# Seven conditioning vectors computed as fp32 products on TensorE instead of multiply-adds on VectorE

## The chip, the cores and the metric

One Trainium2 chip, one core of it. The metric is the device time of one execution in microseconds, smaller is better. A difference is told from no change at about 0.2%, some 4 us here.

## The reference, cut to what matters

One layer of a diffusion backbone over 1024 latent tokens and 256 context tokens, model width 1024. A conditioning vector c and a context vector c_ctx each pass through silu and one matrix `w_ada` (1024 x 9216) and give nine vectors of 1024, which shift, scale and gate the three sub-layers:

```python
def adaln(cond, w, b):
    m = jax.nn.silu(cond) @ w + b
    return [t[..., None, :] for t in jnp.split(m, N_MOD, axis=-1)]

def half_step_ffn(x, mods, g_pre, g_post, w_gu, w_down):
    shift, scale, gate = mods
    h = modulate(rms_norm(x, g_pre), shift, scale)
    g, u = jnp.split(h @ w_gu, 2, axis=-1)
    y = (jax.nn.silu(g) * u) @ w_down
    return x + 0.5 * gate * rms_norm(y, g_post)
...
        mods = adaln(c, w_ada[i], b_ada[i])
        mods_c = adaln(c_ctx, w_ada[i], b_ada[i])
        x = half_step_ffn(x, mods[0:3], ...)
        ctx = half_step_ffn(ctx, mods_c[0:3], ...)
        # mixer: x uses mods[3:6], ctx uses mods_c[3:5]
        x = half_step_ffn(x, mods[6:9], ...)
```

Everything is fp32. A layer of c_ctx needs vectors 0 to 4 only, one of c needs all nine.

## The kernel before

The stages follow each other in time: the first up product of the latent tokens (`g_lat`, to about 512 us), the same of the context (`g_ctx`), the two down products (`d_lat`, `d_ctx`, to about 1060 us), the mixer (in-projection, S5 scans, convolution, out-projection, to about 1510 us), the second up product (`g_lat` again, 1510 to 1920 us) and its down product. An operand of a large product is split into a high and a low fp32r half by ScalarE (a copy) and VectorE (a subtraction); three fp32r products of 512 columns then make one fp32 product. The up products use a seven-product scheme: each of 22 column blocks of the weight takes 7 x 12 matmuls, 1848 in all, and VectorE makes the sums and differences and the low halves that they need.

Vectors 0 and 1 of c are made at the start, by code of their own. The others come from `ada_mods` (line 327), a generator that runs as filling work: `step` (line 122) takes some of its yields at fixed points of a large product and issues them at lower priority. For each vector and each of 8 row blocks of `w_ada` (512 KB, loaded into a ring of five slots named tb, two blocks ahead) `ada_acc` multiplies the block on VectorE by a column of silu(c) (the tile scol) and adds it to an accumulator of 128 x 1024, once for c and once for c_ctx. `ada_col` then sums over partitions: a VectorE transpose in 32 x 32 pieces, a VectorE reduction (the tile red), one small fp32 product with a fixed matrix sel, and four VectorE adds of the bias into the column tile mod. For a gate vector `ada_gate` transposes that column on TensorE and sends it out as a row.

Vectors 1 to 4 are filling work of the first up product, followed by `s5_params` (small VectorE and GpSimd work for the mixer); 5 and 6 of the first down products (`fill56`), 7 of the mixer, 8 of the second up product. The order of the instructions on each engine is set when the program is built, by a list scheduler with its own timing estimates; VectorE is held to the written order only in the opening. Each engine runs its instructions in order, so one that waits holds up those behind it. In the profile nearly all instructions carry line 51, that of a recording helper; they are told apart by tile names. ps is a PSUM tile, w an operand half, wr a raw weight block, z, t and tb are working tiles.

Of the kernel before, what the change touches and what calls it, by code (L numbers as in the profile page):

```python
# [13 lines left out]
OP = mybir.AluOpType  # L14
# [54 lines left out]
class Kernel:  # L69
# [110 lines left out]
    def setup(self):  # L180
# [40 lines left out]
        nc.vector.tensor_copy(self.scol, pt[:, :16])  # L221
        self.ones = self.t(cp, [P, 1], "ones")
        nc.gpsimd.memset(self.ones, 1.0)
        self.modc = {}

    def selector(self):

        nc, cp = self.nc, self.cp
        red = self.t(cp, [P, 32], "red")
        nc.vector.tensor_reduce(  # L230
            red, self.ident.rearrange("p (a j) -> p j a", j=32), axis=AX.X, op=OP.add
        )
        self.sel = self.t(cp, [P, P], "sel")
        for a in range(4):
            nc.vector.tensor_copy(self.sel[:, 32 * a : 32 * a + 32], red)
# [46 lines left out]
    def ada_col(self, acc, mod, cond):  # L282
        nc = self.nc
        tmp = self.ta()
        nc.vector.transpose(tmp, acc)
        red = self.t(self.cp, [P, 32], f"red{mod}_{cond}")
        nc.vector.tensor_reduce(
            red, tmp.rearrange("p (b j) -> p b j", j=32), axis=AX.X, op=OP.add
        )
        self.td_(tmp)  # L290
        yield
        pt = self.ps()
        nc.tensor.matmul(pt[:, :32], self.sel, red, start=True, stop=True)
        col = self.t(self.cp, [P, KT], f"mod{mod}_{cond}")
        for q in range(4):
            r = slice(32 * q, 32 * q + 32)
            self.add(
                col[r, :],
                pt[r, :32].rearrange("p (k q) -> p q k", q=4)[:, q, :],
                self.b_ada(mod)[r, :],  # L300
            )
        self.modc[mod, cond] = col
        yield
# [23 lines left out]
    def ada_mods(self, plan, look=2):  # L327
# [3 lines left out]
        for p, (n, kt) in enumerate(seq):  # L331
# [4 lines left out]
            if kt == 0:  # L336
                accs = [self.ta() for _ in conds]
            w = ws.pop(0)
            for a, cond in zip(accs, conds):
                self.ada_acc(a, w, kt, cond)  # L340
            self.td_(w)
            yield
            if kt == KT - 1:
                self.td_(*accs)
                for a, cond in zip(accs, conds):
                    yield from self.ada_col(a, mod, cond)
# [1266 lines left out]
    def run(self):  # L1613
# [102 lines left out]
        self.selector()  # L1716
# [12 lines left out]
        def fill():  # L1729
            for _ in range(FW):  # L1730
# [6 lines left out]
                (4, (1, 0), scales4),  # L1737
            ])
# [43 lines left out]
        def fill56():  # L1782
            for _ in range(DW):
                yield
# [248 lines left out]
SF = (15, 1)  # L2033
TY = 4
FC = 2
DW = 0
FW = 34
FN = 3
UN2 = 3
# [47 lines left out]
```

## Time and profile before

| | us |
|---|---|
| median of 3 runs (2123.9 to 2125.89) | 2124.05 |
| the profiled execution's own time | 2125.93 |
| span of its trace | 2124.2 |
| TensorE matmul busy in the span | 1925.3 (91%) |
| VectorE busy | 1636.0 (77%) |
| ScalarE busy | 817.0 (38%) |

PE is TensorE, PEld its weight loads, DVE VectorE, ACT ScalarE, POOL GpSimd, SP the queue that issues nearly all DMAs. The busy time of PE counts the modelled end of each matmul, so that 91% does not say how much room TensorE has; that is read from the number of matmuls in a stretch and their spacing. A matmul whose operands are plain fp32 leaves two records in the trace, an fp32r one leaves one; a TensorE transpose leaves one.

### The profile page before, as it was taken

What the parts mean: (1) busy time and instruction counts of PE and PEld (TensorE: products, weight loads), DVE (VectorE), ACT (ScalarE), POOL (GpSimd) and SP (SyncE); (2) the same over time, 40 slices, a digit from 0 to 9 for tenths busy, and PEclk for the clock granted to TensorE, in tenths of its full rate; (3) what the DMA queues carried; (4) which work ended last, traced back from release to release, by engine and by line L of the source; (5) the groups of instructions that cost most, each with busy time, mean ns of one, the idle gap of its engine ahead of it and who ended that gap; (6) DMA issues with size and microseconds to landing.
All of it is one profiled execution on the core that took longest, in us unless ns stands there. A gap on an engine that the chain in (4) does not pass through costs nothing.

```text
span 2124.2 us, 25468 instructions
## 1 busy us (share of the span) xinstructions
PE 1925.3 (91%) x9018; PEld 1594.7 (75%) x9018; DVE 1636.0 (77%) x2813; ACT 817.0 (38%) x1416; POOL 229.5 (11%) x136
## 2 busy tenths in 40 slices
PE   5779998898899988999997779998899999998997
PEld 4568776686899866877886668886688888886876
DVE  6689998998766699598549998478875555579867
ACT  5433322333343333566531113347233333333543
POOL 0000000041337100000003552010000000000000
PEclk9889999999999999999999899999899999999999
DMA  8347552344579969367684433233552322267754
GB/s 299 95 145 245 160 184 84 88 150 139 172 241 264 320 226 339 128 229 279 186 235 174 153 127 114 72 104 114 182 175 79 99 80 90 70 226 250 243 169 168
DMA packets 338444, 366.21 MB, mean 172 GB/s; under 512 B 43216, under 2 KB 250764, under 8 KB 338316
## 3 DMA queue, kind: packets, MB, share of 16 engines
q1 hardware_dynamic: 336012, 356.19, 51.6%
q10 hardware_dynamic: 2304, 8.39, 1.0%
q8 instruction: 71, 1.16, 0.2%
q14 instruction: 57, 0.47, 0.1%
HBM read 299.22 MB, written 67.35 MB: 173 GB/s over the span
## 4 chain that ended last, share of the span: by engine, by line
PE 54%; DVE 29%; DMA 8%; issue 4%; ACT 2%; POOL 2%; SPq 1%; DVEq 0%; ACTq 0%; POOLq 0%
PE ps L51 54%; DVE t L51 10%; DVE z L51 6%; DVE w L51 5%; DVE tb L51 5%; DMA wr<-in_ffn_w_down 2%; DMA tb<-in_w_ada 2%; POOL z L51 1%; SPq L51 1%; DMA wr<-in_ffn_w_gu 1%; DMA z<-in_w_ada 1%; ACT z L51 1%; ACT w L51 1%; DMA wr<-t2d 1%; ACT t L51 0%
## 5 line engine op out<-in xcount | busy, mean ns | idle before, releaser
L51 PE MATMUL ps<-z,w 128*128 128x512 f32 (+1 forms) x5712 | 1245.9, 379 | 94.4 <-ACT w L51 46.1
L51 PEld LDWEIGHTS ps<-z,w 128*128 128x128 f32 x5712 | 1020.8, 194 | 296.1 <-ACT w L51 52.5
L51 PE MATMUL ps<-w,w 128*128 128x512 f32 x1848 | 439.3, 397 | 29.9 <-DVE w L51 23.9
L51 PEld LDWEIGHTS ps<-w,w 128*128 128x128 f32 x1848 | 348.4, 191 | 117.5 <-DVE w L51 35.0
L51 ACT ACTIVATE w<-wr 128x512 fp32r<-128x512 f32 (+1 forms) x308 | 228.9, 747 | 378.8 <-PE ps L51 287.0
L51 DVE TENSOR_TENSOR w<-wr,w 128x512 fp32r<-128x512 f32 (+1 forms) x302 | 268.6, 894 | 91.1 <-ACT w L51 83.6
L51 ACT ACTIVATE w<-t 128x512 fp32r<-128x512 f32 x264 | 160.2, 626 | 294.0 <-DVE t L51 255.6
L51 DVE TENSOR_TENSOR w<-t,w 128x512 fp32r<-128x512 f32 x264 | 181.1, 699 | 40.9 <-ACT w L51 40.6
L51 DVE TENSOR_TENSOR t<-t,ps 128x512 f32<-128x512 f32 x150 | 102.2, 683 | 66.0 <-PE ps L51 65.6
L51 ACT ACTIVATE w<-z 128x512 fp32r<-128x512 f32 x132 | 83.3, 631 | 161.1 <-PE ps L51 158.4
L51 DVE TENSOR_TENSOR w<-z,w 128x512 fp32r<-128x512 f32 x132 | 90.8, 688 | 48.0 <-ACT w L51 47.8
L51 ACT ACTIVATE t<-ps 128x512 f32<-128x512 f32 (+2 forms) x135 | 73.7, 548 | 99.7 <-PE ps L51 98.0
L51 DVE TENSOR_TENSOR z<-z,z 128x512 fp32r<-128x512 f32 (+3 forms) x127 | 103.8, 852 | 9.6 <-ACT z L51 5.8
L51 DVE SCALAR_TENSOR_TENSOR tb<-tb,scol 128x1024 f32<-128x1024 f32 x77 | 97.9, 1280 | 8.6 <-DMA tb<-in_w_ada 8.4
L51 DVE TENSOR_TENSOR t<-wr 128x512 f32<-128x512 f32 x126 | 85.4, 685 | 16.7 <-DMA wr<-in_ffn_w_gu 11.1
L51 POOL TENSOR_TENSOR z<-z,z 128x1024 f32<-128x1024 f32 x24 | 85.4, 3576 | 76.4 <-PE ps L51 39.8
L51 ACT ACTIVATE t<-z 128x1024 bf16<-128x1024 f32 (+3 forms) x132 | 75.2, 605 | 44.3 <-DVE z L51 32.1
L51 ACT ACTIVATE t<-t 128x512 f32<-128x512 f32 (+1 forms) x81 | 50.6, 625 | 104.1 <-DVE t L51 100.1
L51 PE MATMUL ps<-z,t 128*128 128x512 f32 x384 | 87.8, 389 | 1.1 <-ACT t L51 1.1
L51 PEld LDWEIGHTS ps<-z,t 128*128 128x128 f32 x384 | 72.0, 188 | 16.4 <-ACT t L51 1.5
L51 POOL TENSOR_TENSOR tb<-tb 128x512 f32<-128x512 f32 x24 | 33.8, 1422 | 451.3 <-DVE w L51 431.0
L51 ACT ACTIVATE z<-z 128x512 fp32r<-128x512 f32 (+2 forms) x76 | 47.9, 672 | 78.6 <-DVE z L51 72.5
(124 smaller groups left out, 1447.6 us busy)
## 6 DMA issues: line engine op xcount, KB each, us to landing
wr<-in_ffn_w_gu SPq DMA_DIRECT2D x156, 512.0 KB, 4.1
wr<-in_ffn_w_down SPq DMA_DIRECT2D x242, 256.0 KB, 4.4
tb<-in_w_ada SPq DMA_DIRECT2D x64, 512.0 KB, 5.0
sd<-z SPq DMA_DIRECT2D x44, 512.0 KB, 4.8
z<-sd SPq DMA_DIRECT2D x88, 256.0 KB, 5.6
z<-in_w_ada SPq DMA_DIRECT2D x24, 512.0 KB, 6.1
wr<-in_ffn_w_down SPq DMA_DIRECT2D x22, 512.0 KB, 3.6
wr<-in_w_in SPq DMA_DIRECT2D x20, 512.0 KB, 4.0
```

The lines of the kernel that those rows point to most:

```text
L51: r = f(*a, **kw)
```

## The change

Vectors 1 to 4 of c_ctx and 2 to 8 of c are no longer summed on VectorE. A new tile `srep` holds, for each of the 8 row blocks, silu(c) and silu(c_ctx) side by side, repeated 16 times to 32 columns. For each block of `w_ada` TensorE makes four fp32 products of 256 columns, with those 32 columns as the stationary operand; the four write to partitions 0, 32, 64 and 96 of one PSUM tile, so that each uses another group of 32 columns of the array, and accumulate over the 8 blocks. One product serves c and c_ctx at once. `ada_col` copies the result to SBUF on ScalarE, transposes it twice on TensorE and adds the bias in one VectorE instruction per vector. The transposes of 1024 columns, the reductions and `sel` are gone, and with `fill56` and the filling work of the mixer vectors 5, 6 and 7 move into the filling work of the first up product, ahead of `s5_params`. Eight blocks of each of these eight vectors are 256 products there; vector 8 has 32 in the second up product.

```diff
--- before.py
+++ after.py
@@ -219,20 +219,14 @@
         self.tr(pt[:, :16], srow, 16)
         self.scol = self.t(cp, [P, 16], "scol")
         nc.vector.tensor_copy(self.scol, pt[:, :16])
+        self.srep = self.t(cp, [P, KT, 32], "srep")
+        nc.scalar.activation(
+            self.srep.rearrange("p k (n c) -> p n c k", c=2),
+            pt[:, :16].rearrange("p (c k) -> p c k", c=2).unsqueeze(1).to_broadcast([P, 16, 2, KT]), AF.Copy,
+        )
         self.ones = self.t(cp, [P, 1], "ones")
         nc.gpsimd.memset(self.ones, 1.0)
         self.modc = {}
-
-    def selector(self):
-
-        nc, cp = self.nc, self.cp
-        red = self.t(cp, [P, 32], "red")
-        nc.vector.tensor_reduce(
-            red, self.ident.rearrange("p (a j) -> p j a", j=32), axis=AX.X, op=OP.add
-        )
-        self.sel = self.t(cp, [P, P], "sel")
-        for a in range(4):
-            nc.vector.tensor_copy(self.sel[:, 32 * a : 32 * a + 32], red)
 
     def consts(self):
         nc, i, cp = self.nc, self.i, self.cp
@@ -279,27 +273,21 @@
         else:
             self.stt(acc, w, s, acc, OP.mult, OP.add)
 
-    def ada_col(self, acc, mod, cond):
-        nc = self.nc
-        tmp = self.ta()
-        nc.vector.transpose(tmp, acc)
-        red = self.t(self.cp, [P, 32], f"red{mod}_{cond}")
-        nc.vector.tensor_reduce(
-            red, tmp.rearrange("p (b j) -> p b j", j=32), axis=AX.X, op=OP.add
-        )
-        self.td_(tmp)
+    def ada_col(self, pt, mod, conds):
+        rows = self.t2([P, 256])
+        self.nc.scalar.activation(rows, pt[:, :256], AF.Copy)
         yield
         pt = self.ps()
-        nc.tensor.matmul(pt[:, :32], self.sel, red, start=True, stop=True)
-        col = self.t(self.cp, [P, KT], f"mod{mod}_{cond}")
-        for q in range(4):
-            r = slice(32 * q, 32 * q + 32)
+        for b in range(2):
+            self.tr(pt[:, b * P : b * P + P], rows[:, b * P : b * P + P], P)
+        for cond in conds:
+            col = self.t(self.cp, [P, KT], f"mod{mod}_{cond}")
             self.add(
-                col[r, :],
-                pt[r, :32].rearrange("p (k q) -> p q k", q=4)[:, q, :],
-                self.b_ada(mod)[r, :],
+                col.rearrange("p (j b) -> p j b", b=2),
+                pt[:, : 2 * P].rearrange("p (b j r) -> p j b r", b=2, j=4)[:, :, :, cond],
+                self.b_ada(mod).rearrange("p (j b) -> p j b", b=2),
             )
-        self.modc[mod, cond] = col
+            self.modc[mod, cond] = col
         yield
 
     def ada_scale(self, mod, cond, k):
@@ -334,16 +322,17 @@
                 q, k = seq[p + len(ws)]
                 ws.append(self.ada_load(plan[q][0], k, self.ta()))
             if kt == 0:
-                accs = [self.ta() for _ in conds]
+                pt = self.ps()
             w = ws.pop(0)
-            for a, cond in zip(accs, conds):
-                self.ada_acc(a, w, kt, cond)
+            for j in range(4):
+                self.nc.tensor.matmul(
+                    pt[32 * j : 32 * j + 32, :256], self.srep[:, kt, :], w[:, 256 * j : 256 * j + 256],
+                    start=kt == 0, stop=kt == KT - 1,
+                )
             self.td_(w)
             yield
             if kt == KT - 1:
-                self.td_(*accs)
-                for a, cond in zip(accs, conds):
-                    yield from self.ada_col(a, mod, cond)
+                yield from self.ada_col(pt, mod, conds)
                 if done:
                     yield from done() or ()
                 yield
@@ -1713,7 +1702,6 @@
         go(S1)
         for _ in h:
             pass
-        self.selector()
         self.floor = (self.last, self.anchor)
         self.nc.order(False, *G0)
         self.nc.order(True, *G1)
@@ -1735,6 +1723,9 @@
                 (2, (1, 0), gates1),
                 (3, (1, 0), None),
                 (4, (1, 0), scales4),
+                (5, (0,), lambda: self.ada_gate(5, 0, 1, False, 2)),
+                (6, (0,), None),
+                (7, (0,), lambda: self.ada_scale(7, 0, 2)),
             ])
             yield from self.s5_params()
 
@@ -1779,15 +1770,6 @@
 
         gate = self.gate_tile(1)
 
-        def fill56():
-            for _ in range(DW):
-                yield
-            yield from self.ada_mods([
-                (5, (0,), lambda: self.ada_gate(5, 0, 1, False, 2)),
-                (6, (0,), None),
-            ])
-
-        self.fill = fill56()
         self.pace = True
         ys = []
         hm = []
@@ -1841,7 +1823,6 @@
         src = self.ucd.rearrange("(g h) t c -> t h g c", h=H)
         for t in range(T8):
             self.load(u[t * H : t * H + H, :, CL:], src[t])
-        self.fill = self.ada_mods([(7, (0,), lambda: self.ada_scale(7, 0, 2))], 1)
         self.pace = False
         yc, part = [], []
         cover = itertools.chain(self.conv(mhi, mlo, yc), self.out_conv(yc, part))
@@ -2033,7 +2014,6 @@
 SF = (15, 1)
 TY = 4
 FC = 2
-DW = 0
 FW = 34
 FN = 3
 UN2 = 3
```

On TensorE, in the first up product, before: the first vector's small product (of red and sel) stands among the 512-column products.

```order
L51 MATMUL ps_1275<-z_653,w_1353 128x512 x2
L51 MATMUL ps_1464<-red_1_321_1462,sel_894 128x32
L51 MATMUL ps_1418<-z_594,w_1334 128x512
L51 MATMUL ps_1418<-z_620,w_1334 128x512 x3
L51 MATMUL ps_1418<-z_625,w_1334 128x512 x3
```

The same place with the change: the first blocks of the first vector, products of a tb block and srep.

```order
L51 MATMUL ps_1233<-z_849,w_1230 128x512 x3
L51 MATMUL ps_1310<-tb_72,srep_173 32x256
L51 MATMUL ps_1233<-z_853,w_1230 128x512
L51 MATMUL ps_1310<-tb_72,srep_173 32x256
L51 MATMUL ps_1233<-z_853,w_1230 128x512
...
L51 MATMUL ps_1377<-z_353,w_1285 128x512 x2
L51 MATMUL ps_1310<-tb_72,srep_173 32x256 x12
L51 MATMUL ps_1429<-z_596,w_1336 128x512 x3
```

The 288 new products stand in 164 runs: 139 of a single product between two of 512 columns, and 25 of 2 to 12 in a row, so that 124 follow directly on another of their kind. In the first up product there are 256 in 141 runs, between its 447th and 1292nd product of 512 columns; in the second 32 in 23.

On VectorE, in the first up product, before: multiply-adds of blocks of `w_ada` (tb with scol) stand between the operand splits (w).

```order
L51 SCALAR_TENSOR_TENSOR tb_72<-tb_72,scol_171 128x1024 x2
L51 TENSOR_TENSOR t_287_1176<-t_287_1176,ps_1145 128x512
L51 TENSOR_TENSOR t_299_1270<-wr_3_74,wr_4_75 128x512
L51 TENSOR_TENSOR w_1253<-wr_3_74,w_1253 128x512
L51 SCALAR_TENSOR_TENSOR tb_72<-tb_72,scol_171 128x1024
L51 TENSOR_TENSOR w_1272<-t_299_1270,w_1272 128x512
L51 SCALAR_TENSOR_TENSOR tb_72<-tb_72,scol_171 128x1024
```

The same place with the change, where the first vector's bias is added.

```order
L51 TENSOR_TENSOR z_1422<-t_305_1332,t_301_1283 128x512
L51 TENSOR_TENSOR t_325_1503<-wr_4_75 128x512
L51 TENSOR_TENSOR mod_1_323_1486<-ps_1483,cols_189 128x8
L51 SCALAR_TENSOR_TENSOR mod_1_323_1486<-mod_1_323_1486,cols_189 128x8
L51 TENSOR_TENSOR w_1505<-t_325_1503,w_1505 128x512
```

Of a vector only two instructions of 8 columns are left there.

On SP's queue, in the first up product, with the change: loads of `w_ada` blocks into tb ahead of the next raw weight blocks wr. A load into tb waits until TensorE has read the slot's last block.

```order
L51 DMA wr_5_76<-in_ffn_w_gu 128x8x128
L51 DMA tb_72<-in_w_ada 128x1024 x8
L51 DMA wr_3_74<-in_ffn_w_gu 128x8x128
L51 DMA wr_4_75<-in_ffn_w_gu 128x8x128
```

Before, VectorE freed these slots, and most of the 24 loads of vectors 5 to 7 stood behind the first up product.

## Rows read from the trace of the kernel before

**Rows 1.** The page: span, busy time of each engine.

```profile
span 2124.2 us, 25468 instructions
PE 1925.3 (91%) x9018; PEld 1594.7 (75%) x9018; DVE 1636.0 (77%) x2813; ACT 817.0 (38%) x1416; POOL 229.5 (11%) x136
```

**Rows 2.** Busy time by stretch: four stretches, with instruction counts.

```profile
core 0: us, PE busy (x) PEld busy (x) DVE busy (x) ACT busy (x) POOL busy (x), PEclk, DMA share, GB/s
158.00:512.00 354.00, 321.22 (x1384) 260.47 (x1382) 328.06 (x605) 114.97 (x200) 33.85 (x24) 0.97 0.49 153
800.00:840.00 40.00, 30.90 (x120) 22.31 (x118) 35.77 (x54) 14.78 (x32) 0.00 (x0) 0.96 1.00 364
1200.00:1206.00 6.00, 1.46 (x9) 1.25 (x9) 5.91 (x9) 0.00 (x0) 3.40 (x3) 0.82 0.78 249
1510.00:1920.00 410.00, 409.41 (x1800) 338.83 (x1801) 257.40 (x399) 149.39 (x257) 0.00 (x0) 1.00 0.39 126
```

**Rows 3.** The chain that ended last: two pieces (start us, us, what).

```profile
499.32 8.36 DMA tb<-in_w_ada
...
1510.59 407.13 PE ps L51 x1789
```

**Rows 4.** VectorE's groups in 158 to 512 us (busy us, mean ns, idle before).

```profile
L51 DVE SCALAR_TENSOR_TENSOR tb<-tb,scol 128x1024 f32<-128x1024 f32 x58 | 73.6, 1279 | 4.5 <-DMA tb<-in_w_ada 4.3
L51 DVE STREAM_TRANSPOSE tb<-tb 128x1024 f32<-128x1024 f32 x8 | 9.9, 1239 | 0.0
L51 DVE TENSOR_REDUCE red<-tb 128x32 f32<-128x1024 f32 x8 | 9.7, 1214 | 0.0
L51 DVE TENSOR_SCALAR tb<-tb,scol 128x1024 f32<-128x1024 f32 x9 | 6.7, 748 | 5.0 <-DMA tb<-in_w_ada 5.0
L51 DVE TENSOR_TENSOR mod<-ps,cols 32x8 f32<-32x8 f32 x32 | 5.1, 159 | 0.4
```

**Rows 5.** Waits of TensorE in 158 to 512 us (us, times, longest).

```profile
PE ps L51 <- ACT w L51: 18.8, 3, 8.2
PE ps L51 <- DVE mod L51: 6.3, 1, 6.3
PE ps L51 <- DVE w L51: 4.7, 4, 2.4
```

**Rows 6.** Timeline of TensorE: plain fp32 products of 160 columns, S5 stage.

```profile
1124.76 1.11 PE L51 MATMUL ps<-tb,z 128*128 128x160 f32 x7
```

**Rows 7.** All TensorE records on tb and z tiles (ns min/median/max).

```profile
L51 PE MATMUL ps<-tb,z x192: 270/299/474, 1121.7 to 1299.3; 128*128 128x160 f32 x128, 128*128 128x128 f32 x64
```

**Rows 8.** Timeline of TensorE: a transpose of 32 rows between 512-column products.

```profile
353.06 1.07 PE L51 MATMUL ps<-z,w 128*128 128x512 f32 x4
354.06 0.25 PE L51 MATMUL ps<-ident,t 32*128 32x32 f32 x1
354.23 1.20 PE L51 MATMUL ps<-z,w 128*128 128x512 f32 x4
```

**Rows 9.** The same for a transpose with a stationary operand of 8 columns.

```profile
1682.59 1.07 PE L51 MATMUL ps<-z,w 128*128 128x512 f32 x4
1683.49 0.27 PE L51 MATMUL ps<-ident,mod 128*8 128x128 f32 x1
1683.52 1.17 PE L51 MATMUL ps<-z,w 128*128 128x512 f32 x4
```

**Rows 10.** Timeline of TensorE: plain transposes of 128 columns in a row.

```profile
525.77 1.47 PE L51 MATMUL ps<-ident,z 128*128 128x128 f32 x12
```

**Rows 11.** VectorE's groups in 800 to 840 us.

```profile
L51 DVE SCALAR_TENSOR_TENSOR tb<-tb,scol 128x1024 f32<-128x1024 f32 x6 | 7.7, 1280 | 1.3 <-DMA tb<-in_w_ada 1.3
L51 DVE STREAM_TRANSPOSE tb<-tb 128x1024 f32<-128x1024 f32 x1 | 1.2, 1239 | 0.0
L51 DVE TENSOR_REDUCE red<-tb 128x32 f32<-128x1024 f32 x1 | 1.2, 1207 | 0.0
```

**Rows 12.** VectorE in 1200 to 1208 us: vector 7's transpose.

```profile
L51 DVE STREAM_TRANSPOSE z<-z 128x1024 f32<-128x1024 f32 x1 | 1.2, 1245 | 0.0
```

## The prediction

> **What bounds the kernel now.** I read the page first: TensorE is busy for 91% and VectorE for 77% of the span [rows 1], but a share over the whole span decides nothing here, because the change takes work from VectorE and gives work to TensorE in particular stages. So I went to the busy time by stretch. In the second up product (1510 to 1920 us) TensorE is busy for 409 of 410 us and VectorE for 257: TensorE alone is the bound, and the chain that ended last runs through it without a break, 1789 products in 407.13 us, 0.2276 us each [rows 2, 3]. That spacing is the measure of TensorE's real work in the same product code elsewhere. In 158 to 512 us, most of the first up product, stand 1384 records [rows 2]. Sixteen are of the small products with sel and about five are transposes, perhaps 1.5 us together; the other 1363 x 0.2276 = 310.2 us. So of 354 us TensorE needs about 312 and lacks work (or runs at the lower clock behind a gap; the granted clock is 0.97 there) for **42 us**. VectorE is busy for 328 of the 354. The reader should see two engines that are both nearly full. The multiply-adds, transposes, reductions and bias adds of the vectors are 73.6 + 6.7 + 9.9 + 9.7 + 5.1 = 105 us of VectorE's time there [rows 4]. Taking 105 us off VectorE can give back at most the 42 us, since TensorE's own 312 us remain.
>
> **The change, part by part.** The sum is made against the profiled execution's 2125.93 us, which lies 1.9 us above the median of the runs shown.
>
> *New products in the first up product.* 256 fp32 products of 256 columns. The nearest row is the fp32 product of 160 columns in the S5 stage: seven records in 1.11 us [rows 6]; one record lasts 0.299 us [rows 7], so the spacing is (1.11 - 0.30) / 6 = 0.135 us a record and 0.27 us a product, which has two. If the time goes with the columns that is 0.27 x 256 / 160 = **0.432 us** for 256 columns; if it did not depend on them it would be 0.27, the lower bound. I take 0.432, because an fp32r product has 512 columns in 0.2276 us, about one a tick of the 2.4 GHz level, and the 160-column product takes 4.1 ticks a column. 256 x 0.432 = +110.6 us. That the stationary operand has 32 columns in place of 128 saves nothing by this, as the moving columns set the time.
>
> *What of it is covered.* The products stand where TensorE's queue has 845 products of 512 columns, 192 us of its own; with the new work that is over 300 us. VectorE, rid of 105 us, no longer sets the pace. TensorE's waits in the stretch are for splits by ScalarE and VectorE (18.8 and 4.7 us) and for a mod column (6.3 us) [rows 5]. The longest, 8.2 us, comes where the chain runs through 8.36 us of waiting for a w_ada block [rows 3]; 9.3 us of such waits stand in front of the vectors' instructions on VectorE [rows 4]. These waits go with the multiply-adds. What stays is the gate's transpose behind the mod column, and `s5_params`, which now falls into the last part of the product and fills VectorE there. I take 36 of the 42 us back; bounds 5 (if TensorE now waits for the blocks itself) and 42. **-36.**
>
> *Second up product.* 32 x 0.432 = **+13.8 us**, all on the path, since TensorE is full there and the vector's VectorE work, 7 x 1.28 + 0.75 + 1.24 + 1.21 + 0.64 = 12.8 us by the durations of [rows 4], was hidden behind it.
>
> *Going from 128 columns to groups of 32 and back.* 164 runs, each in and out. Two transposes of the trace bound it. Each stands between two times four products of 512 columns, which alone would take 1.07 + 4 x 0.2276 = 1.98 us. With a transpose that has 32 rows, from 353.06 to 354.23 + 1.20 = 355.43, it is 2.37: 0.39 us for 32 columns that are 0.03 us of work, 0.36 lost [rows 8]. With one that has a stationary operand of 8 columns it is 1683.52 + 1.17 - 1682.59 = 2.10: 0.12, of which the 128 columns themselves are (1.47 - 0.27) / 11 = 0.11 [rows 10], so about 0.02 with rounding [rows 9]. The new products have all rows and few columns, like the second, so I take 0.02: **+3.3 us**; 0.36 is the upper bound and a rival.
>
> *First down products.* In 800 to 840 us TensorE has 120 products, 27.3 us, in 40: 12.7 us are lost. VectorE has 7.7 + 1.2 + 1.2 us, and some 0.6 of bias adds, for vector 6, and DMA is busy for 1.00 of the stretch [rows 2, 11]. Without the vector's work and its loads I take **-8 us** (3 to 12). Vector 5 cost nothing while TensorE was full, and its 8.2 us wait is counted above.
>
> *Mixer.* Vector 7's transpose of 1.2 us, a reduction as long and four adds stand in the S5 scans, where VectorE is busy for 5.91 of 6 us [rows 2, 12]: **-3** (0 to 4). Its multiply-adds lay under full products of TensorE and give nothing.
>
> *The rest.* `selector` goes from VectorE's opening, about -1 us. 18 transposes of 0.11 us [rows 10] come, 24 records of the sel products go: nothing. ScalarE's copies are 9 small ones on an engine that is 38% busy [rows 1]. The loads of vectors 5 to 7 (12 MB) come into a stretch whose DMA share is 0.49 [rows 2]; SP's queue now holds raw weight loads behind loads that wait for TensorE, eight once. Behind such a late weight block stand VectorE's sums and ScalarE's copies of one column block, and then TensorE. VectorE runs ahead by then, so I cost it at nothing; without that cover, some 3 us at each of a few places, 0 to 15 us.
>
> Sum: 110.6 - 36 + 13.8 + 3.3 - 8 - 3 - 1 = **+79.7 us**, 2205.6 on the profiled execution's scale, 2204 on that of the median.
>
> **The rivals.**
>
> *Products that follow each other overlap (column groups run side by side).* 124 products follow directly on another of their kind and use another group. If the first record of each runs beside the second of the one before, 124 x 0.216 = 26.8 us go: **2177**. If runs overlap wholly, 53.6 go: **2150**. No row has two column groups, so nothing in the trace speaks for or against. The order speaks against much of it: 139 of 288 products stand alone between full-width ones. The Trainium skill, "TensorE: Matmul & The Clock Gate", section on packing small matmuls, has column groups run concurrently, 2.38 times faster for three; no run here shows it yet, and by it whole runs would overlap.
>
> *Every change of width empties the array.* Then the 0.36 us of rows 8 holds for each of 164 runs: 59 in place of 3.3 us, **2260**, or **2233** together with the pairwise overlap. Against it: rows 9, where the 8-column operand cost nothing visible. The Trainium skill, "TensorEngine Tiling (Array Packing)", Key Properties, says that a change of tiling mode drains TensorE; rows 8 agree with it for rows, rows 9 do not show it for columns.
>
> *Faster: the products are cheap.* If a 256-column product with 32 stationary columns streamed its columns once, as an fp32r product does, it would take 0.2276 / 2 = 0.114 us, and the sum would be 29.2 - 36 + 3.6 + 3.3 - 12 = -12 us, **2112**. The point from which it decides: 288x = 36 + 12 - 3.3, x = 0.155 us a product. Against it: the 0.27 us that 160 columns take now, measured over 128 stationary columns. Near that point the change would make no difference.
>
> **How the numbers follow.** Chances: no overlap and no drain 0.38 (2204); pairwise overlap 0.22 (2177); whole runs overlap 0.08 (2150); drain alone 0.12 (2260); drain with overlap 0.10 (2233); cheap products 0.07 (2112); no difference 0.03. The predicted time is the first. The likeliest case alone runs from 2190 (more of the down stage given back, all 42 us recovered) to 2220 (weight loads late). The range 2148 to 2250 leaves out the cheap products, no difference, and most of the drain alone, 0.20. A measurement of this kernel tells some 0.2%, 4 us, from no change: faster 0.07, same 0.03, slower 0.90.
>
> **What would show it.** Right: in the first up product TensorE's records lie without gaps, the granted clock near 1.00, VectorE's busy share there down to some 60%, and the stage ends some 75 us later; two records of about 0.216 us spacing for each new product; the second up product is 14 us longer; the waits for tb blocks are gone from VectorE. Wrong: two new products start within a few hundredths of a us of each other (overlap), the next 512-column product starts more than 0.3 us late behind each single one (drain), records of 0.05 to 0.1 us (cheap products), or TensorE waits for w_ada or weight blocks in the first up product, so that little of the 42 us comes back. The prediction falls if a new product costs under 0.2 us or over 0.6 us of TensorE's time.

## The result and the profile after

The changed kernel takes 2250.94 us (2244.19 to 2256.06, four runs) against 2124.97 of the kernel before: ratio 1.0589 [1.0568, 1.0611], slower. The profiled execution took 2251.29 us, 125.4 more than that of before. The forecast was 2204, range 2148 to 2250: direction right, size wrong, and the time just outside the range.

To see where the 125 us came from, the 7056 products of 512 columns, which both kernels have in the same number, serve as milestones. The table gives the start of product number 200, 1800 (near the end of the first up product), 2000 (first down product, behind the context up product), 2800 (later in it), 4800 and 5800 (early and late in the second up product) and 7055 (the last), each less the start of the same number in the kernel before, in us, from the traces. All kernels of this study are in it; they are described below.

| | 200 | 1800 | 2000 | 2800 | 4800 | 5800 | 7055 |
|---|---|---|---|---|---|---|---|
| the change | -4.8 | 74.7 | 110.6 | 101.3 | 102.4 | 120.0 | 125.4 |
| no_groups | -0.4 | 74.7 | 110.4 | 97.5 | 98.8 | 113.0 | 114.4 |
| grouped_runs | 0.2 | 2.4 | 39.5 | 27.9 | 27.5 | 33.8 | 39.3 |
| s5_early | 0.2 | 131.6 | 138.5 | 128.8 | 128.9 | 146.4 | 152.8 |
| run_of_4 | -1.0 | 212.3 | 250.8 | 241.7 | 241.7 | 253.9 | 257.0 |
| run_of_4_s5_early | 1.4 | 268.1 | 268.6 | 261.5 | 259.1 | 271.6 | 272.1 |
| grouped_s5_first | 0.2 | 62.6 | 64.9 | 53.4 | 54.7 | 61.0 | 67.2 |
| fill_4_per_step | -1.9 | 71.4 | 68.7 | 63.1 | 61.7 | 79.2 | 80.5 |
| undo_move | -0.2 | 50.3 | 56.5 | 59.2 | 60.8 | 78.4 | 83.5 |
| move_only | -3.2 | -10.8 | 28.0 | 17.3 | 18.5 | 18.5 | 18.5 |
| move_only_fill4 | 0.8 | 33.0 | 35.1 | 25.1 | 24.5 | 24.3 | 26.6 |
| grouped_fill4_v8 | 0.3 | 15.7 | 15.7 | 7.5 | 10.5 | 10.5 | 11.7 |
| grouped_1_to_4 | -2.4 | -5.7 | -1.2 | 0.9 | -0.4 | -0.4 | 1.5 |

In the first row, 79.5 us come in the first up product up to number 1800, **35.9 from there to number 2000, most of them in the context up product**, -9.3 in the down products, 1.1 up to the second up product, 17.6 in it and 5.4 behind it. The prediction had nothing in the second place. Of the 35.9 us, 6.4 still lie at the end of the first up product, whose number 1840 is 81.1 us late. In the kernel before that product ends at 552 us, not at about 512 as the description of that kernel has it. What the context up product loses is below always the step from 1800 to 2000.

The first two lines answer to [rows 1], the windows below to [rows 2] (busy us and count of PE, PEld, DVE, ACT, POOL, then clock, DMA share, GB/s). The page and the busy time by stretch, changed kernel:

```profile
span 2249.5 us, 26460 instructions
PE 2046.1 (91%) x9588; PEld 1615.0 (72%) x9588; DVE 1510.7 (67%) x2652; ACT 822.8 (37%) x1426; POOL 215.1 (10%) x136
...
158.00:512.00 354.00, 354.00 (x1586) 219.04 (x1585) 137.97 (x255) 89.25 (x158) 0.00 (x0) 1.00 0.46 147
540.00:632.00 92.00, 81.54 (x358) 65.03 (x357) 88.72 (x172) 36.89 (x63) 29.90 (x18) 0.96 0.47 137
632.00:655.00 23.00, 22.48 (x181) 21.96 (x179) 21.54 (x26) 8.10 (x12) 11.16 (x8) 1.00 0.99 261
655.00:682.00 27.00, 0.10 (x1) 0.13 (x1) 15.28 (x15) 2.97 (x5) 10.26 (x4) 0.58 0.69 248
682.00:698.00 16.00, 15.69 (x88) 15.51 (x89) 7.63 (x4) 2.52 (x4) 10.14 (x4) 0.63 0.12 34
1640.00:2045.00 405.00, 405.00 (x1777) 323.00 (x1776) 227.26 (x355) 140.91 (x244) 0.00 (x0) 1.00 0.37 120
```

In 158 to 512 us TensorE is now busy throughout at a granted clock of 1.00, so its 42 us of room are gone, as forecast. VectorE is busy for 138 us in place of 328. Some 105 us of the difference were the vectors. Some 45 us are sums and splits of the up product itself, because the same stretch now holds 1050 products of 512 columns in place of 1361. The rest, some 40 us, is `s5_params`, which has left the stretch, as GpSimd's 0.00 in place of 33.85 us shows. It turns up in 540 to 632 us, where VectorE is busy for 88.7 of 92 us and TensorE lacks work again, and runs on to 655 to 682 us, where TensorE does nothing. TensorE's timeline there, changed kernel (start, us, what; in brackets the idle time before and its releaser):

```profile
648.85 5.63 PE L51 MATMUL ps<-z,w 128*128 128x256 f32 x45
681.90 0.61 PE L51 MATMUL ps<-z,z 128*128 128x32 f32 x2 [27.42 <-DVE z L51]
682.32 1.31 PE L51 MATMUL ps<-ident,z 128*128 128x128 f32 x5
683.27 4.58 PE L51 MATMUL ps<-z,w 128*128 128x256 f32 x23
```

What it waits for is read from the chain of waits of the same kernel (start, us, what):

```profile
659.52 5.23 DMA brd<-tb
...
664.81 6.81 DMA z<-brd
...
671.64 10.12 DVE z L51 x4
...
681.78 3.27 DVE z L51
```

`s5_params` ends by sending a table to DRAM (brd); the S5 preparation reads it back and works on it on VectorE, and small products (128x32) of that work stand in TensorE's order among those of the context up product. So 5 + 7 + 10 us of transfers and VectorE work lie on the path. The issue of the two transfers shows by how much the chain moved. First the kernel before, then the change (ns min/median/max, first and last start):

```profile
L51 SPq DMA_DIRECT2D brd<-tb x1: 326/326/326, 498.9 to 498.9; - x1
L51 SPq DMA_DIRECT2D z<-brd x1: 1441/1441/1441, 550.1 to 550.1; - x1
```

```profile
L51 SPq DMA_DIRECT2D brd<-tb x1: 423/423/423, 659.5 to 659.5; - x1
L51 SPq DMA_DIRECT2D z<-brd x1: 326/326/326, 664.8 to 664.8; - x1
```

Before, brd went out some 50 us ahead of the end of the first up product (551 us, number 1840 of the milestones); now it goes 28 us behind it (632). It is 161 us later while the product is 81 us later. VectorE's timeline has the work on the table that is read back, first in the kernel before, then in the change:

```profile
562.53 9.33 DVE L51 TENSOR_TENSOR z<-z,z 128x1024 f32<-128x1024 f32 x3
```

```profile
671.64 16.38 DVE L51 TENSOR_TENSOR z<-z,z 128x1024 f32<-128x1024 f32 x6 [11.65 <-DMA z<-brd]
```

Before, it began some 10 us behind the end of the product, and TensorE came to the small products at 579.7 us without a wait for them. In the change it begins 38 us behind the product; TensorE is done at 654.5 us with all that stands ahead of the small products in its order, and waits.

After the wait the granted clock is 0.63 for 16 us, a mean of its two levels, 1.2 and 2.4 GHz, and the 256-column products stand (4.58 - 0.56) / 22 = 0.183 us apart where ahead of it they stood (5.63 - 0.36) / 44 = 0.120: by the clock some 16 x 0.37 = 6 us more. From number 1800 to 2000 all of TensorE's waits sum to 46.9 us in the change, 27.7 of them for z, and to 14.8 in the kernel before. So 32 us of waits and some 6 of clock stand against the 35.9 measured.

The new products themselves, changed kernel, TensorE's timeline at singles and at a run of twelve, then all their records:

```profile
176.59 0.62 PE L51 MATMUL ps<-tb,srep 128*32 128x256 f32 x2
177.14 0.49 PE L51 MATMUL ps<-z,w 128*128 128x512 f32 x1
177.57 0.62 PE L51 MATMUL ps<-tb,srep 128*32 128x256 f32 x2
...
191.81 1.07 PE L51 MATMUL ps<-z,w 128*128 128x512 f32 x4
192.81 1.50 PE L51 MATMUL ps<-tb,srep 128*32 128x256 f32 x24
194.24 2.11 PE L51 MATMUL ps<-z,w 128*128 128x512 f32 x8
...
L51 PE MATMUL ps<-tb,srep x576: 379/379/403, 176.6 to 1781.7; 128*32 128x256 f32 x192
```

From one single to the next, with one 512-column product between, are 177.57 - 176.59 = 0.98 us, less 0.23 for that product: **0.75 us for a single product**, not 0.43. The twelve take 194.24 - 191.81 - 4 x 0.2276 = **1.52 us, 0.127 each**. Taken so from start to start for each run between 512-column products, 139 singles have a median of 0.745, runs of four 0.66, of eight 1.09, of twelve 1.52. All 288 together take 123.3 us, 107.3 in the first up product and 16.1 in the second; the prediction had 110.6 + 13.8 + 3.3 = 127.7. So the price of the products came out right as a sum, and wrong in two of its parts. (The 256 in the first up product belong to vectors 0 to 7: vector 0 of c_ctx, which the description of the change leaves out, is among them.)

The lengths split the price. From four to eight to twelve a run grows by 0.43 us for every four products, which is the prediction's price of a single one; 0.66 - 0.43 = 0.23 us are paid once a run. What a single pays depends on its group: of the 41 that go to the first group of 32 columns, 34 take 0.64 to 0.65 us, of the 98 that go to the others 94 take 0.74 to 0.76.

### The profile page after: what moved, and what is told of

Its sections match the earlier page's. It is cut to its first block, busy times and chain, and to the rows that moved or that the text cites. A ratio compares the mean times of both kernels' runs of the same rounds, so it can differ in the third digit from the quotient of the medians.

```text
span 2249.5 us, 26460 instructions
## 1 busy us (share of the span) xinstructions
PE 2046.1 (91%) x9588; PEld 1615.0 (72%) x9588; DVE 1510.7 (67%) x2652; ACT 822.8 (37%) x1426; POOL 215.1 (10%) x136
## 4 chain that ended last, share of the span: by engine, by line
PE 63%; DVE 20%; DMA 8%; issue 3%; ACT 2%; SPq 2%; POOL 1%; DVEq 0%; ACTq 0%; POOLq 0%
PE ps L51 63%; DVE t L51 8%; DVE z L51 6%; DVE w L51 3%; DMA wr<-in_ffn_w_down 2%; SPq L51 2%; DMA wr<-in_ffn_w_gu 1%; DVE tb L51 1%; DMA z<-in_w_ada 1%; POOL tb L51 1%; ACT z L51 1%; DMA z<-sd 1%; DMA wr<-t2d 1%; ACT w L51 1%; ACT t L51 1%
## 5 line engine op out<-in xcount | busy, mean ns | idle before, releaser
L51 PE MATMUL ps<-z,w 128*128 128x512 f32 (+1 forms) x5712 | 1278.9, 380 | 80.9 <-ACT w L51 28.4
L51 PEld LDWEIGHTS ps<-w,w 128*128 128x128 f32 x1848 | 350.1, 191 | 114.5 <-DVE w L51 39.1
L51 DVE TENSOR_TENSOR w<-wr,w 128x512 fp32r<-128x512 f32 (+1 forms) x302 | 259.8, 863 | 112.9 <-ACT w L51 106.2
L51 DVE TENSOR_TENSOR t<-t,ps 128x512 f32<-128x512 f32 x150 | 102.4, 684 | 149.9 <-PE ps L51 149.7
L51 DVE TENSOR_TENSOR z<-z,z 128x512 fp32r<-128x512 f32 (+3 forms) x127 | 117.9, 965 | 22.4 <-DMA z<-brd 11.7
L51 PE MATMUL ps<-tb,srep 128*32 128x256 f32 x576 | 108.4, 388 | 0.0
L51 POOL TENSOR_TENSOR tb<-tb 128x512 f32<-128x512 f32 x24 | 39.3, 1652 | 602.7 <-DVE w L51 575.4
L51 DVE TENSOR_TENSOR z<-t,ps 128x512 f32<-128x512 f32 (+1 forms) x52 | 29.7, 572 | 93.2 <-PE ps L51 93.2
```

Of the source, the lines that this page charges most:

```text
L51: r = f(*a, **kw)
```

## The experiments

Theory: (1) a run of products pays some 0.3 us for going into the column groups and back, and inside a run the four groups work side by side; both were missed and cancel. (2) The 36 us of the context up product come from `s5_params`, which three more vectors ahead of it make late. Rivals: the products cost by their columns alone; a single one is dear because of fp32 or its weight load, not because of its width; the context up product is late for other reasons.

**s5_early**

```diff
+            ])
+            yield from self.s5_params()
+            yield from self.ada_mods([
                 (5, (0,), lambda: self.ada_gate(5, 0, 1, False, 2)),
                 (6, (0,), None),
                 (7, (0,), lambda: self.ada_scale(7, 0, 2)),
             ])
-            yield from self.s5_params()
```

> The same work as the change, but s5_params stands ahead of vectors 5 to 7 in the filling work, as it stood ahead of them before. Theory A (the late end of s5_params is the second half of the miss): in the changed kernel the context up product waits 27.4 us at 654 us for a VectorE sum that hangs on the broadcast of brd, issued at 659.5 us after the first up product had ended; before it was issued at 498.9 us. With s5_params early that wait and the low clock behind it go: 2251 - 29 = 2222 us, 2216 to 2230. Theory B (the context up product is late because it is crowded by what the vectors leave behind, whichever piece comes last): another piece of filling work takes the place of the wait, 2245 to 2255.

2275.53 us, 1.0728 [1.0702, 1.0753]: slower than the change. The context up product does lose only 6.9 us (table, 1800 to 2000), but 56.9 more were lost in front of it. TensorE's waits in 158 to 720 us (us, times, longest):

```profile
PE ps L51 <- DMA tb<-in_w_ada: 48.7, 2, 45.0
```

`s5_params` takes all five slots of the tb ring while it lasts. The load of vector 5's first block stands behind it, and that block's product had been placed in TensorE's order well ahead. Theory A's number failed because a new wait took the place; the mechanism for the old wait is supported, not yet isolated.

**run_of_4** and **run_of_4_s5_early**

```diff
+            with self.tc.tile_critical():
-            for j in range(4):
-                self.nc.tensor.matmul(
+                for j in range(4):
+                    self.nc.tensor.matmul(
...
```

> The same work as the change, but the four products of a block follow each other directly on TensorE (72 runs of four in place of 164 runs of mixed length). Theory A (a run pays for going into the 32-column groups and back out, and the four of a block run side by side): a run of four took TensorE 0.77 us in the changed kernel, a single product about as much, so 64 runs cost 49 us in the first up product in place of some 116, and 8 cost 6 us in the second in place of 18: -67 - 12, 2251 - 79 = 2172 us, if the 27 us wait of the context up product stays. Theory B (TensorE's time goes with the products' columns, 0.43 us each, as the prediction had it): no difference, 2240 to 2255. In between, some 2200, if the first up product has no such gain because VectorE or the loads then set its pace.

> Both edits together: runs of four, and s5_params ahead of vectors 5 to 7. Theory A of both: 2251 - 79 - 29 = 2143 us, 2135 to 2160. If the late s5_params was not the cause of the wait, some 2172; if the runs were not, some 2222.

2383.24 us, 1.1238 [1.1212, 1.1263], and 2404.09, 1.1334 [1.1306, 1.1362]: both far off. TensorE's timeline in run_of_4 shows why it is no test of the first theory:

```profile
205.42 0.64 PE L51 MATMUL ps<-tb,srep 128*32 128x256 f32 x8 [0.44 <-issue]
211.06 1.08 PE L51 MATMUL ps<-tb,srep 128*32 128x256 f32 x8 [5.00 <-PEq L327]
216.78 1.08 PE L51 MATMUL ps<-tb,srep 128*32 128x256 f32 x8 [4.63 <-PEq L327]
```

The critical section (line 327) keeps TensorE's own sequencer, here for some 5 us each time; in 158 to 700 us there are 26 such waits, 111.4 us in all (PEq), and 35.9 us more that the trace puts down to the issue. The order had to be made another way. For the second theory the pair does say something: the context up product loses 38.5 us in run_of_4 and 0.5 in run_of_4_s5_early, though there, too, the first up product is longer by more than that.

**no_groups**

```diff
+        self.srep = self.t(cp, [P, KT * 112 + 16], "srep")
...
-                    pt[32 * j : 32 * j + 32, :256], self.srep[:, kt, :], w[:, 256 * j : 256 * j + 256],
+                    pt[j // 2][:, 256 * (j % 2) : 256 * (j % 2) + 256], self.srep[:, 112 * kt : 112 * kt + P],
+                    w[:, 256 * j : 256 * j + 256], ...
```

> The same vectors with a stationary operand of 128 columns in place of 32 and no column groups: 288 products of the same 256 columns, each of the full width of the array, in the same places among the others, into two PSUM tiles for each vector; nothing can run side by side and the width never changes. Theory A (single products cost 0.75 to 0.86 us because the width changes before and after): 288 x 0.432 = 124 us of TensorE in place of some 134, a little faster than the change, 2235 to 2247 us, with 0.43 us for a single product between two of 512 columns. Theory B (a single one costs that because of the change from fp32r to fp32 and back, or of the load of its operand, whatever the width): 0.75 us each without any overlap, 288 x 0.75 = 216, 2251 + 82 = 2330 us.

2242.17 us, 1.0582 [1.0555, 1.0609], as theory A had it; the rival's 2330 is out. TensorE's timeline, no_groups:

```profile
205.41 0.59 PE L51 MATMUL ps<-tb,srep 128*128 128x256 f32 x2
205.66 0.58 PE L51 MATMUL ps<-z,w 128*128 128x512 f32 x1
206.07 0.59 PE L51 MATMUL ps<-tb,srep 128*128 128x256 f32 x2
```

206.07 - 205.41 - 0.2276 = 0.43 us for a single product of the full width, among the same fp32r products (median of 136 singles: 0.433). It is the prediction's 0.432, and the second up product is 14.2 us longer here (table, 4800 to 5800), the prediction's 13.8; the 0.745 of a single product in a group is 0.31 more. So the 0.31 us go with the column groups, not with fp32 or the load of the operand, which has 128 columns here. A narrow operand that stays in one group was not tried. The interval holds the change's 1.0589: as the change orders its products, four column groups save nothing that can be told from noise (all new products together take 114.2 us of TensorE here, 123.3 there).

**grouped_runs**

```diff
-    def ada_mods(self, plan, look=2):
+    def ada_mods(self, plan, look=4):
...
-                self.nc.tensor.matmul(
+                with self.tc.issue_after(self.nc.tensor.prev):
+                    self.nc.tensor.matmul(
...
+            self.tail4 = self.nc.tensor.prev
...
-                nc.tensor.matmul(pt, wh, h, start=first and k == 0, stop=False, **on)
+                with self.tc.issue_after(self.tail4) if self.tail4 and k == 0 else nullcontext():
+                    nc.tensor.matmul(pt, wh, h, start=first and k == 0, stop=False, **on)
```

> The work of the change, with TensorE's order alone changed: each fp32 product is issued behind the TensorE instruction written before it, and the next block of 512-column products behind the last fp32 product, so that the products of one filling step stand together: 36 runs (15 of twelve, 6 of eight, 12 of four, three others) in place of 164; w_ada blocks are loaded four ahead in place of two. No critical section, which in the earlier run of fours made TensorE's sequencer wait some 5 us each. Theory A (0.31 us for a run's change of width, the four groups side by side): by the changed kernel's own runs, 1.52 us for twelve, 1.09 for eight, 0.66 for four, the 36 runs take 15 x 1.52 + 6 x 1.09 + 12 x 0.66 + 2 = 39 us in place of 123 counted: 2251 - 84 = 2167 us if the 27 us wait of the context up product stays, 2155 to 2190. Theory B (the products' columns count): 2240 to 2255. Theory C (standing together is itself what made the run of fours slow): above 2300.

2165.84 us, 1.0195 [1.0170, 1.0220]: 2167 was expected. TensorE's timeline, grouped_runs:

```profile
281.67 1.52 PE L51 MATMUL ps<-z,w 128*128 128x512 f32 x6
283.12 1.50 PE L51 MATMUL ps<-tb,srep 128*32 128x256 f32 x24
284.56 1.65 PE L51 MATMUL ps<-z,w 128*128 128x512 f32 x6
```

The run of twelve takes 284.56 - 281.67 - 6 x 0.2276 = 1.52 us as before; there are 15 of them, and all runs, 35 in the trace, together take 39.1 us in place of 123.3, with the same 288 products. Number 1800 of the first up product comes 2.4 us later than in the kernel before (change: 74.7), the second up product is 6.3 us longer (17.6). The runs are shorter by 84.2 us and the kernel by 85, so the loads four blocks ahead, part of the same edit and not tried alone, can have had little share. This settles the first theory. The late `s5_params` stays, with a wait of 35.8 us on VectorE's z (37.1 in the table).

**grouped_s5_first**

```diff
             for _ in range(FW):
                 yield
+            yield from self.s5_params()
             yield from self.ada_mods([
...
             ])
-            yield from self.s5_params()
```

> As the grouped runs, with s5_params as the first piece of the filling work, ahead of all vectors, so that neither its end nor its five tb slots can be late for anything behind it. Theory A (the 27 us wait of the context up product comes from the late s5_params): 2167 - 29 = 2138 us, 2120 to 2150, and no wait over 5 us in the context up product. Theory B (the stage is late for another reason): as the grouped runs, 2160 to 2190.

2189.38 us, 1.0301 [1.0272, 1.0329]: missed again. The context up product loses 2.3 us now, so the wait is gone, but TensorE waits for w_ada as in s5_early, here for vector 1's first block:

```profile
PE ps L51 <- DMA tb<-in_w_ada: 58.9, 2, 54.9
```

**fill_4_per_step**

```diff
-FN = 3
+FN = 4
```

> The change with one number edited: each filling step of the first up product issues four pieces of filling work in place of three, so that the whole filling work, s5_params at its end, comes out some quarter earlier. GpSimd's first piece of s5_params stands at 577 us in the changed kernel and brd is sent at 659.5; a quarter of the some 430 us since the filling began is 110 us, so brd would go at about 550, ahead of the end of the first up product at 632. Theory A (the wait of the context up product comes from the late s5_params alone): that wait goes, 2251 - 29 = 2222 us, 2212 to 2232. Theory B (any order leaves a wait of that size, as the two kernels with s5_params ahead showed with w_ada in its place): 2240 to 2290.

2207.92 us, 1.0404 [1.0375, 1.0433], some 14 us better than expected, and a little below theory A's range. brd is issued 98 us sooner than in the change, ahead of the end of the first up product, and TensorE's longest wait for z in 158 to 720 us, fill_4_per_step, is 0.6 us:

```profile
L51 SPq DMA_DIRECT2D brd<-tb x1: 423/423/423, 561.6 to 561.6; - x1
...
PE ps L51 <- DVE z L51: 0.6, 1, 0.6
```

The context up product now loses -2.7 us against 35.9, with the order of the filling work unchanged: the second theory holds. The other few us are TensorE's: it has 134 runs and 105.7 us of new products here, but `s5_params` is inside the first up product again, whose number 1800 comes only 3.3 us sooner (number 1840: 9.7).

**move_only** and **move_only_fill4**

```diff
                 (4, (1, 0), scales4),
+                (5, (0,), lambda: self.ada_gate(5, 0, 1, False, 2)),
+                (6, (0,), None),
+                (7, (0,), lambda: self.ada_scale(7, 0, 2)),
             ])
...
-        self.fill = fill56()
...
-        self.fill = self.ada_mods([(7, (0,), lambda: self.ada_scale(7, 0, 2))], 1)
```

and, in the second kernel, FN = 4 as above.

> The kernel before with one part of the change: vectors 5 to 7 are made in the first up product, still by VectorE. VectorE is busy for 328 of the 354 us there, and gets 24 multiply-adds of 1.28 us and 3 x 3.8 us of transposes, reductions and adds: the first up product ends some 40 us later. Theory A (s5_params behind three more vectors ends after the product, whichever engine sums them): the context up product also waits, 20 to 30 us; with the 11 us given back by the down products and 3 by the mixer 2121 + 40 + 25 - 14 = 2172 us, 2160 to 2190. Theory B (s5_params is late only where TensorE makes the vectors): 2121 + 40 - 14 = 2147 us.

> Vectors 5 to 7 in the first up product, all by VectorE, and four pieces of filling work per step. The move alone took 2145 us with a 39.8 us wait of the context up product and 11 us given back by the down products; its first up product ended 11 us earlier than before, since s5_params had left it. Theory A: with s5_params back inside, the wait goes and the 11 us too: 2145 - 40 + 11 = 2116 us, 2105 to 2128. Theory B (VectorE is full there, and s5_params adds its length): 2140 to 2165.

2145.33 us, 1.0101 [1.0067, 1.0135], and 2153.99, 1.0138 [1.0095, 1.0181]. With VectorE's sums the move alone makes brd late (584.8 us) and TensorE wait. Its waits in 158 to 720 us, first move_only, then move_only_fill4:

```profile
PE ps L51 <- DVE z L51: 40.5, 2, 39.8
```

```profile
PE ps L51 <- DVE red L51: 30.3, 5, 13.5
```

So the wait belongs to the move, whichever engine sums. My 2172 for move_only was off by the first up product, expected 40 us longer and in fact 10.8 shorter, since the displaced `s5_params` freed VectorE for the sums. That the time is near the 2147 of theory B is chance: its kernel would have no wait. With four pieces per step the wait goes, `s5_params` is back inside, and the product is 33 us longer: VectorE is full there (busy for 335 of the 354 us from 158 to 512), as its rival said.

**undo_move**

```diff
-                (5, (0,), lambda: self.ada_gate(5, 0, 1, False, 2)),
-                (6, (0,), None),
-                (7, (0,), lambda: self.ada_scale(7, 0, 2)),
             ])
             yield from self.s5_params()
...
+        self.fill = self.ada_mods([
+            (5, (0,), lambda: self.ada_gate(5, 0, 1, False, 2)),
+            (6, (0,), None),
+        ])
...
+        self.fill = self.ada_mods([(7, (0,), lambda: self.ada_scale(7, 0, 2))], 1)
```

> The change without the move: all vectors on TensorE, but 5 and 6 are filling work of the first down products and 7 of the mixer, as before. Theory A: s5_params is on time, so the context up product doesn't wait; the first up product has 160 new products, some 0.45 us each, 72 us less 37 of room = +35; the down products get 64, some 35 us less 10 for what VectorE and TensorE's gaps there give = +20 (10 to 30); the mixer 32, +8 (0 to 14); the second up product +18: 2121 + 81 = 2202 us, 2185 to 2220. Theory B (the wait of the context up product has nothing to do with the moved vectors): another 29 us, 2231.

2208.73 us, 1.0395 [1.0374, 1.0417], within theory A. brd goes at 548.0 us and the context up product loses 6.2 us. The places differ from the expectation: 50.3 us in the first up product (35 expected), 2.7 in the down products (20 expected), where TensorE had room.

**grouped_1_to_4** and **grouped_fill4_v8**: attempts at a faster kernel. The first has vectors 1 to 4 (and 0 of c_ctx) on TensorE in grouped runs, all else as before; the second the grouped runs, FN = 4 and vector 8 back on VectorE.

```diff
-            yield from self.ada_mods([(8, (0,), lambda: self.ada_gate(8, 0, 2, True, 3))])
+            yield from self.ada_mods_v([(8, (0,), lambda: self.ada_gate(8, 0, 2, True, 3))])
```

(`ada_mods_v` is the old VectorE code.)

> Only vectors 1 to 4 on TensorE, in grouped runs; vectors 5 to 8 on VectorE in their old places, s5_params where it was. 160 products in 18 runs take some 22 us of TensorE by the runs of the changed kernel, and VectorE is rid of 105 us in the first up product. Theory A (TensorE's 42 us without work there are for want of VectorE): 31 of them came back in the grouped runs, 2121 + 22 - 31 = 2112 us, 2100 to 2125. Theory B (the moved vectors gave the rest, and VectorE's sums cost little there): 2125 to 2145.

> The grouped runs, with four pieces of filling work per step (s5_params earlier) and vector 8 made by VectorE again. Theory A: of the 2166 us the 35.8 us wait of the context up product goes, and the 6.5 us by which the second up product was longer; VectorE's part of s5_params, now inside the first up product, finds room there: 2166 - 36 - 6 = 2124 us, 2112 to 2135, about that of the kernel before. Theory B (the wait only moves): 2150 to 2170.

2127.58 us, 1.0008 [0.9989, 1.0027], no difference from the kernel before and in theory B's range; and 2134.21, 1.0059 [1.0035, 1.0083], slower than the kernel before, within theory A's range. In grouped_1_to_4 the 160 products take 21.5 us of TensorE, and VectorE is busy for 235 of the 354 us:

```profile
158.00:512.00 354.00, 341.32 (x1693) 266.07 (x1692) 234.93 (x509) 118.26 (x206) 36.09 (x24) 0.99 0.48 151
```

The first up product ends 5.7 us sooner, and the next stages take that back. TensorE's room there was only partly for want of VectorE; what else holds it was not tried. No kernel of the study beats the one before.

## Why the prediction missed, step by step

**The step that failed** is the sentence that `s5_params` "now falls into the last part of the product and fills VectorE there", with no price. The whole of that piece was moved behind 24 more blocks, and it ends in a chain (a DMA out, a DMA in, VectorE work, products in the middle of the context up product) that TensorE's products ahead of them no longer hide, once VectorE's part begins 38 us behind the up product in place of 10. It measured 35.9 us of the change, out of a miss of 46. The rivals had no such case: the waits they named were for blocks and weights. Neither VectorE's order nor the waits of [rows 5] could show it; the issue of brd at 498.9 us could have, beside 24 moved blocks at three pieces a step.

**New products: 127.7 us forecast, 123.3 measured, by two errors that cancel.** *The price by columns, 0.432,* is right: 0.433 in no_groups. *Switching at 0.02 us,* taken from rows 9, is wrong: 0.745 - 0.433 = 0.31 for most singles, near the 0.36 of rows 8, which was my upper bound. The singles take 99.8 us, and 139 x 0.433 = 60.2 without switching; that is 40 us, with some 6 for the longer runs 46, where 3.3 were put. *No overlap* is wrong too: every four products of a run add 0.43 us, 0.11 each, a quarter of 0.432, and 12 x 0.433 = 5.2 us shrink to 1.5. In all the overlap saves some 288 x 0.433 + 46 - 123.3 = 47 us. Of my rivals "drain with pairwise overlap", 2233, came nearest in mechanism; whole-run overlap with the drain was not among them. The Trainium skill, "TensorEngine Tiling (Array Packing)", Key Properties, has a change of tiling mode drain TensorE. The runs agree that such a change costs time, 0.31 us for a single product going in and out; I let rows 9 outweigh it. The Trainium skill, "TensorE: Matmul & The Clock Gate", section on packing small matmuls, gives 2.38 for three groups. The runs of twelve, with four groups, show 5.2 / 1.5 = 3.4.

**-36 of TensorE's room:** -28, the right kind, a little small. Numbers 400 to 1800 took 367.9 us before, 47.8 of them beyond 1400 x 0.2276 = 318.6 and 1.5 of small work. In the change they take 447.4; less 318.6, 1.5 and the 107.3 of new products, 20.0 are left. Some 14 of them lie behind the last new product (number 1292), most where `s5_params` now fills VectorE (540 to 632 us in the windows). 107.3 - 27.8 = 79.5 us for the first up product; 78 were forecast.

**Second up product, +13.8:** 17.6, since its 32 products stand in 23 runs; 6.3 in grouped_runs. **Down products, -8:** -9.3, within 3 to 12. **Mixer, -3:** +1.1 from number 2800 to 4800; nothing came back. **Opening, -1:** -4.8 at number 200, but -1.9 to 1.4 in the other kernels without `selector` and -3.2 in move_only, which has it, so not counted as its gain. **Behind the second up product, 0:** +5.4, at one place of the last down product, where TensorE waits 6.9 us for VectorE's splits in place of 2.1; why the splits are late there was not tried.

**Signs named ahead.** Of the signs of being right, the clock near 1.00, the records without gaps and the stage some 75 us later are there. Two signs of being wrong are there too: the next 512-column product is 0.31 us late behind 101 of the 139 singles (0.21 behind the others), and in the run of twelve the records start in sets of four, some 7 ns apart. By its own limits, 0.2 and 0.6 us, the prediction of the price falls, at 0.75 us for a single product and 0.13 in a run of twelve; only the mean, 123.3 / 288 = 0.43, fits. VectorE's share "down to some 60%" was 39%, the trace's hint that more than the vectors had left the stretch.

In fill_4_per_step, where the late chain is mended, the change costs 80.5 us by the last milestone (85 by the medians); the sum of the prediction was 79.7. That nearness owes as much to the cancelling errors as to the terms.

## What to carry to other kernels

When filling work is put ahead of another piece in an ordered stream, price the last consumer of the displaced piece: when does its last output leave, how long is the chain of transfers behind it, and which in-order engine has instructions of that chain among its own. Small products in column groups pay per run and per set of four, not per product: here 0.2 to 0.3 us for going in and out and 0.43 for up to four side by side, so keep those of several blocks together or stay at full width. And mending one wait by moving a piece forward can make another, where the piece holds buffers that the rest loads into: twice here, for 45 and 55 us.

## What the runs showed of the hardware that was not expected

Going from 128 columns to a group of 32 and back costs a single product 0.31 us (0.745 against 0.433), yet a transpose with an 8-column operand showed nearly nothing in [rows 9]; what tells the two apart was not tried. The first of the four groups costs less than the others: 0.21 us for most of its singles, 0.23 for the runs of four, eight and twelve, which all begin in it, while the runs of three, which begin in the second, take 0.76 us, 0.1 more than the runs of four (0.66). Why the groups differ is open. Four products in four groups took the time of one (0.43 us more for each four). After 27 us without work TensorE's granted clock was 0.63 for 16 us, between its two levels. A critical section around four products kept TensorE's sequencer for some 5 us.
